# Strassen-like f16 matmul: the fault flag summed by a one-column TensorE product instead of a GpSimd all-reduce, with all instructions in a newly searched order

## The chip, the cores and the metric

One core of one Trainium2 chip. The metric is the device time of the whole program in microseconds (us). Engines are named PE (TensorE), DVE (VectorE), ACT (ScalarE), POOL (GpSimd) and SP (SyncE, which issues the DMAs). Before the change three runs gave a median of 1486.29 us (1484.29 to 1486.7).

## The reference

```
B, S, D = 8, 2048, 2048        # x: (8, 2048, 2048) f32, w: (2048, 2048) f32
cs = np.cumsum(x, axis=1)
diff = cs - concatenate([zeros, cs[:, :-1, :]], axis=1)
return np.matmul(diff, w)
```

The difference of a running sum is the input again, so what is computed is x·w: 16384 rows of 2048 by a 2048×2048 matrix, with f32 results.

## The kernel before

The kernel multiplies in f16 and adds in f32. The rows of x are cut into 128 tiles of 128 rows. The first 4 tiles are done as plain products while w is loaded and cast; the sums and differences of w's blocks that the rest needs are made after that. The other 124 tiles go in 31 **groups** of 4 (`group`, L554 to L648), and each group is a multiplication of 2×2 blocks with seven products instead of eight. Six of them, P1 to P5 and P7, are split once more in the same way (class `Seven`), into seven slots, P1.0 to P1.6 and so on. The sixth block product is done whole, in eight parts (P6g and P6h, L525 to L541). A **piece** is one slot or one such part: 4 matmuls of 128×128 by 128×512, in the source lines L435 to L448 (`quarter`) or L531. A group has 50 pieces.

Around the pieces of a group stand:

- on SP: loads of the next group's x (L134, into three stages of F), transposes of the cast tiles by DMA (`turn`, L162), and stores of finished results (`put`, L510, and in halves in the last group, L522);
- on ACT: casts of x to f16 (`narrow`), sums of absolute values for the range check (`weigh`, L152), and copies from PSUM (L118): in each of P1 to P5 and P7 `first` copies the bank of slot 0 to the bank in which slot 3 goes on, `out2` and `out4` copy partial results to SBUF, and `keep` copies a product into a result tile;
- on DVE (all in L115): the f16 sums of x blocks (S1g to S4h for the group, `s1` to `s4` in each product), the f16 sums of w blocks (`in1.Q1` and so on, 128×2048), and the f32 adds of PSUM banks onto results, such as C11h+P2.1 or C21h+P7.0;
- on POOL (also L115): f32 adds of SBUF tiles, 12 per group, such as P2.last, P7.last and C22g+C21.0. All 372 are of one form, 128×512.

In slot 1 a product needs `s1` and its `Q1`; in slot 2 it needs `s2`, and the copy `first` must have read the bank, because slot 2 adds to the bank that `first` copies from. P1.first overwrites a bank that C21h+P7.0 of the group before still reads. P5.first overwrites a bank that the C11 adds (C11g+P2, C11h+P2) still read.

The helpers don't issue at once. `record` (L97) notes each instruction with a label; `emit` (L103 to L111) sorts all of them by group number × 100000 + a place, and issues them in that order through `after` (L85), engine by engine. Each engine works its own queue in order. The places stand in the table `places` (L715 to L1155), one part for each of the first three and last three groups and one, with the key None, for groups 3 to 27. So that table is the schedule of all five engines.

After the last group, seven small DVE instructions (flag1 to flag7, L687 to L697) judge from the range sums whether f16 was enough. Flag8 (L702) makes the greatest value over all 128 partitions with GpSimd's `partition_all_reduce`; flag9 (L708, DVE) turns it into one number. L1159 loads that number into a register, and L1160 branches on it: when it is above 0 a general path with scaled inputs computes everything again. In these runs the general path is not taken.

Of the kernel before, what the change touches and what calls it, by code (L numbers as in the profile page):

```python
# [10 lines left out]
def kernel(  # L11
# [6 lines left out]
    nc = tc.nc  # L18
    P = 128
# [8 lines left out]
    f16 = mybir.dt.float16  # L28
# [30 lines left out]
    flags = tiny[:, 16:32]  # L59
    told = const.tile([P, 2, END - PLAIN], f16, name="told")  # L60
# [122 lines left out]
    record("zeros", "dve", lambda: nc.vector.memset(zeros, 0.0))  # L183
    record("ones", "dve", lambda: nc.vector.memset(number[0], 1.0))
# [495 lines left out]
    fault = tiny.bitcast(i32)[:, 40:41]  # L680

    def dve(label, ask):
        record(label, "dve", ask)

    def judge():
# [12 lines left out]
        dve("flag7", lambda: ins.tensor_scalar(flags[:, 3:4], seen_w, WLEAST, None, ALU.is_ge))  # L698
        record(
            "flag8",  # L700
            "pool",
            lambda: nc.gpsimd.partition_all_reduce(  # L702
                flags[:, 4:6], flags[:, 2:4], P, bass_isa.ReduceOp.max
# [4 lines left out]
            lambda: ins.tensor_scalar(  # L708
                fault, flags[:, 4:5], 1.0, flags[:, 5:6], ADD, ALU.is_gt
            ),  # L710
# [13 lines left out]
            'first x.0.0': -460890, 'ones': -457444, 'numbers': -438705,  # L724
            'numbers turned': -433943, 'first x.0.3': -422332, 'first x.1.0': -413922,
# [510 lines left out]
```

## Time and profile before

| | |
|---|---|
| median of three runs | 1486.29 us |
| profiled execution | 1483.12 us, of which the span is 1481.3 us |
| PE busy | 1430.6 us (97%), 6542 matmuls |
| DVE busy | 1328.8 us (90%) |
| ACT busy | 1043.6 us (70%) |
| POOL busy | 568.5 us (38%) |
| mean granted clock of PE | 0.991 |

The span runs from the first instruction to the last. The profile gives each engine's busy time, a picture of the span in 40 slices, the waits (who waited, for whom, total, times and longest), and rows in order of time: start in us, length in us, engine, line, operation, output, inputs, how many instructions the row joins, and in brackets the idle time before it with what ended it. A row "x4" of PE is one piece. Ends of matmuls are modelled and overlap the next start a little, so the pace of PE is read from the starts.

### The profile page before, as it was taken

The page shows a single profiled execution, that of the slowest core. Times are in us where ns is not written, and L with a number is a line of the kernel's source. Part 1 is how long each engine was busy: PE and PEld are TensorE (multiplying, and loading weights), DVE is VectorE, ACT ScalarE, POOL GpSimd, SP SyncE. Part 2 cuts the span into 40 slices and gives each one's busy share as a digit, 9 for nine tenths or more (in the row PEclk, how much of TensorE's full clock was granted, in tenths as well). Part 3 has the DMA queues.
Part 4 walks back from the last instruction along what each step waited for, and adds up shares of the span by engine and source line. Part 5 has one row for each costly group of instructions (what it writes and reads, how often), then busy time and mean ns, then how long its engine had stood idle before and what let it go on. Part 6 is the DMA issues. An engine that isn't in the chain of part 4 may idle for free. (4 is left out here: it accounts for less than half of the span.)

```text
span 1481.3 us, 20480 instructions
## 1 busy us (share of the span) xinstructions
PE 1430.6 (97%) x6542; PEld 630.3 (43%) x6542; DVE 1328.8 (90%) x2105; ACT 1043.6 (70%) x1716; POOL 568.5 (38%) x377
## 2 busy tenths in 40 slices
PE   8989999999999999999999999999999999999995
PEld 4434344444444444444444444444444444444442
DVE  2889889999999999999999999999999999998994
ACT  5976867767767777777777776777776776776761
POOL 0014432345443345443345443245443345443333
PEclk9999999999999999999999999999999999999997
DMA  9998788888888998878989988989888899878862
GB/s 359 355 220 246 211 221 236 245 245 230 236 227 244 242 256 232 238 229 231 248 248 244 224 232 233 230 254 245 227 231 236 245 249 240 226 223 231 242 190 93
DMA packets 343791, 351.63 MB, mean 237 GB/s; under 512 B 270976, under 2 KB 270976, under 8 KB 343680
## 3 DMA queue, kind: packets, MB, share of 16 engines
q1 hardware_dynamic: 343680, 350.29, 84.8%
q8 instruction: 52, 0.85, 0.2%
q14 instruction: 59, 0.48, 0.1%
HBM read 150.99 MB, written 134.22 MB: 193 GB/s over the span
## 5 line engine op out<-in xcount | busy, mean ns | idle before, releaser
L115 POOL TENSOR_TENSOR arena<-arena 128x512 f32<-128x512 f32 x372 | 567.9, 1542 | 901.3 <-DVE arena L115 427.0
L118 ACT COPY arena<-b 128x512 f32<-128x512 f32 x729 | 405.3, 589 | 247.0 <-PE b L438 179.4
L438 PE MATMUL b<-W,x 128*128 128x512 f16 x2108 | 517.3, 380 | 8.4 <-ACT arena L118 5.3
L438 PEld LDWEIGHTS <-x 128*128 128x128 f16 x3224 | 313.3, 98 | 412.1 <-issue 40.4
L115 DVE TENSOR_TENSOR arena<-W 128x2048 f16<-128x2048 f16 (+1 forms) x287 | 352.0, 1227 | 9.5 <-PE b L438 5.8
L438 PE MATMUL b<-W,arena 128*128 128x512 f16 x1364 | 338.4, 380 | 11.9 <-ACT b L118 9.5
L438 PEld LDWEIGHTS <-arena 128*128 128x128 f16 x1984 | 187.6, 98 | 271.5 <-DVE arena L115 36.9
L118 ACT CAST F<-F 128x1024 f16<-128x1024 f32 x248 | 257.1, 1047 | 57.6 <-DMA F<-in_x_dram 55.5
L438 PE MATMUL b<-arena,x 128*128 128x512 f16 x1116 | 282.4, 380 | 14.1 <-ACT arena L118 12.7
L115 DVE TENSOR_TENSOR arena<-arena,b 128x512 f32<-128x512 f32 x372 | 249.7, 680 | 30.0 <-PE b L438 11.9
L152 ACT ACTIVATE F<-F 128x1024 f16<-128x1024 f16 x248 | 264.4, 1067 | 1.0
L115 DVE TENSOR_TENSOR x<-x,x 128x1024 f16<-128x1024 f16 x372 | 227.9, 626 | 33.3 <-PE b L438 26.6
L531 PE MATMUL b<-W,x 128*128 128x512 f16 x992 | 240.3, 380 | 0.6 <-ACT F L152 0.4
L118 ACT COPY b<-b 128x512 f32<-128x512 f32 x186 | 106.5, 573 | 105.6 <-DVE arena L115 65.1
L438 PE MATMUL b<-arena 128*128 128x512 f16 x620 | 159.2, 379 | 3.0 <-DVE arena L115 2.4
L115 DVE TENSOR_TENSOR b<-b,arena 128x512 f32<-128x512 f32 x217 | 150.4, 693 | 4.6 <-PE b L438 1.2
L531 PEld LDWEIGHTS <-x 128*128 128x128 f16 x992 | 96.9, 98 | 118.2 <-DVE x L115 1.7
L115 DVE TENSOR_TENSOR arena<-b,arena 128x512 f32<-128x512 f32 x155 | 106.2, 686 | 27.9 <-PE b L438 17.7
L115 DVE TENSOR_TENSOR arena<-arena,x 128x512 f16<-128x512 f16 x124 | 80.5, 649 | 1.1
L115 DVE TENSOR_TENSOR x<-x 128x512 f16<-128x512 f16 x124 | 64.7, 522 | 2.4 <-PE b L438 1.2
L115 DVE TENSOR_TENSOR arena<-x,arena 128x512 f16<-128x512 f16 x124 | 64.1, 517 | 2.1 <-PE b L438 1.9
L115 DVE TENSOR_TENSOR arena<-x 128x512 f16<-128x512 f16 x124 | 58.4, 471 | 1.8
(40 smaller groups left out, 309.8 us busy)
## 6 DMA issues: line engine op xcount, KB each, us to landing
F<-in_x_dram SPq DMA_DIRECT2D x248, 512.0 KB, 5.1
out_dram<-arena SPq DMA_DIRECT2D x240, 512.0 KB, 5.2
W<-in_w_dram SPq DMA_DIRECT2D x32, 512.0 KB, 9.0
out_dram<-arena SPq DMA_DIRECT2D x32, 256.0 KB, 3.0
W<-in_x_dram SPq DMA_DIRECT2D x16, 256.0 KB, 7.7
x<-F SPq DMA_TRANSPOSE x248, 3.4
```

What stands on the lines that cost most here:

```text
L115: record(label, engine, lambda: on.tensor_tensor(dst, p, q, op))
L118: record(label, "act", lambda: nc.scalar.copy(to, p))
L152: return nc.scalar.activation(other, data, ABS, accum_out=m)
L438: said = nc.tensor.matmul(to, a[:, ds(k * P, P)], b[:, k, :], start=(start and k == 0), stop=(k == 3), skip_group_check=True,)
L531: said = nc.tensor.matmul(to[n], half(t, 0)[:, k, :], T2[k][:, n, :], start=False, stop=(k == KH - 1), skip_group_check=True,)
```

## The change

It has two parts. First, the flag: a vote of each partition is worked out on DVE from flags 2 and 3 (-256 for a partition that has seen a fault, +1 for one whose w was large enough). One PE matmul with a column of ones adds the 128 votes into one element of PSUM bank `xy[1][0]`. Flag9 compares this sum with 0.5. GpSimd takes no part in it, and `fault` is made on partition 0 only.

```
+    one = tiny.bitcast(f16)[:, 84:85]
...
+    record("one", "dve", lambda: nc.vector.memset(one, 1.0))
...
-    fault = tiny.bitcast(i32)[:, 40:41]
+    fault = tiny.bitcast(i32)[0:1, 40:41]
+    vote = tiny.bitcast(f16)[:, 86:87]
+    votes = xy[1][0]
...
+        dve(
+            "vote",
+            lambda: ins.tensor_scalar(
+                vote, flags[:, 2:3], -2.0 * P, flags[:, 3:4], MUL, ADD
+            ),
+        )
         record(
             "flag8",
-            "pool",
-            lambda: nc.gpsimd.partition_all_reduce(
-                flags[:, 4:6], flags[:, 2:4], P, bass_isa.ReduceOp.max
+            "pe",
+            lambda: nc.tensor.matmul(
+                votes[0:1, 0:1], one, vote, start=True, stop=True, skip_group_check=True
             ),
         )
         dve(
             "flag9",
-            lambda: ins.tensor_scalar(
-                fault, flags[:, 4:5], 1.0, flags[:, 5:6], ADD, ALU.is_gt
-            ),
+            lambda: ins.tensor_scalar(fault, votes[0:1, 0:1], 0.5, None, ALU.is_lt),
         )
```

Second, the whole table `places` is replaced. Before there were 6464 recorded instructions, now there are 6466: two more on DVE, one more on PE and one fewer on POOL. Two of the table's lines as they were:

```
-            'zeros': -4646627, 'warm.0': -4646625, 'warm.1': -4646623, 'warm.2': -4646621,
-            'warm.3': -4646618, 'warm.4': -4646616, 'warm.5': -4646614, 'warm.6': -4646612,
```

What this moves, at three places.

POOL's whole queue of the main path, before. L115 are its adds, L702 is flag8; "ISA" is an instruction that the compiler puts ahead of a change of kind, and x366 joins equal rows:

```order
L115 ISA
L115 TENSOR_TENSOR arena<-arena 128x512 x366
L702 ISA
L702 ISA tiny<-tiny 128x2
L115 ISA
L115 TENSOR_TENSOR arena<-arena 128x512 x6
L1159 TENSOR_LOAD tiny
L1160 COMPARE_AND_BRANCH
```

And now, with the two rows ahead of it (all lines of the helpers have moved down by one):

```order
L1236 MEMSET const-uint8-127 128x1
L1247 UNCONDITIONAL_BRANCH
L116 ISA
L116 TENSOR_TENSOR arena<-arena 128x512 x372
L1175 TENSOR_LOAD tiny
L1176 COMPARE_AND_BRANCH
```

The reduction stood between the adds of the last group, with six of them behind it. Now the 372 adds follow each other.

DVE at the hand-over from one middle group to the next, before. In order of the rows: P4.s4, the add P4.middle, C21g+P4.0, P1.s2 of the next group, C21h+P7.0, in1.Q1 (from W), C21g+P4.1, P1.s4, P1.middle:

```order
L115 TENSOR_TENSOR x_67<-x_67 128x512
L115 TENSOR_TENSOR b_81<-b_79,arena 128x512
L115 TENSOR_TENSOR arena<-arena,b_80 128x512
L115 TENSOR_TENSOR arena<-arena,x_62 128x512
L115 TENSOR_TENSOR arena<-arena,b_74 128x512
L115 TENSOR_TENSOR arena<-W 128x2048
L115 TENSOR_TENSOR arena<-arena,b_81 128x512
L115 TENSOR_TENSOR arena<-x_62,arena 128x512
L115 TENSOR_TENSOR b_75<-b_77,arena 128x512
```

Now, in order: P4.s4, C21g+P4.0, in1.Q1, C21h+P7.0, P1.s2, C21g+P4.1, P1.s3, C21h+P4.0, P1.middle, P1.s4:

```order
L116 TENSOR_TENSOR x_67<-x_67 128x512
L116 TENSOR_TENSOR arena<-arena,b_80 128x512
L116 TENSOR_TENSOR arena<-W 128x2048
L116 TENSOR_TENSOR arena<-arena,b_74 128x512
L116 TENSOR_TENSOR arena<-arena,x_62 128x512
L116 TENSOR_TENSOR arena<-arena,b_81 128x512
L116 TENSOR_TENSOR arena<-x_62,x_64 128x512
L116 TENSOR_TENSOR arena<-arena,b_78 128x512
L116 TENSOR_TENSOR b_75<-b_77,arena 128x512
L116 TENSOR_TENSOR arena<-x_62,arena 128x512
```

C21h+P7.0 (the row with b_74) and in1.Q1 stood behind P1.s2 and stand ahead of it now. On PE, P1.2 stood ahead of P1.1 (P2.0, P1.2, P1.1, P1.3) and stands behind it now (P2.0, P1.1, P1.2, P1.3).

DVE at the entry to P5 of a middle group, before. In order: C11h+P2.1, C11g+P2.1, C11h+P2.0, S1h, P5.s1, P5.s2, S2h, in5.Q1:

```order
L115 TENSOR_TENSOR arena<-arena,b_81 128x512
L115 TENSOR_TENSOR arena<-arena,b_79 128x512
L115 TENSOR_TENSOR arena<-arena,b_80 128x512
L115 TENSOR_TENSOR x_68<-x_68,x_69 128x1024
L115 TENSOR_TENSOR arena<-x_68 128x512
L115 TENSOR_TENSOR arena<-arena,x_66 128x512
L115 TENSOR_TENSOR x_64<-x_68,x_64 128x1024
L115 TENSOR_TENSOR arena<-W 128x2048
```

Now, in order: C11h+P2.1, S1h, S2h, P5.s1, C11g+P2.1, C11h+P2.0, P5.s2, in5.Q1:

```order
L116 TENSOR_TENSOR arena<-arena,b_81 128x512
L116 TENSOR_TENSOR x_68<-x_68,x_69 128x1024
L116 TENSOR_TENSOR x_64<-x_68,x_64 128x1024
L116 TENSOR_TENSOR arena<-x_68 128x512
L116 TENSOR_TENSOR arena<-arena,b_79 128x512
L116 TENSOR_TENSOR arena<-arena,b_80 128x512
L116 TENSOR_TENSOR arena<-arena,x_66 128x512
L116 TENSOR_TENSOR arena<-W 128x2048
```

S1h, S2h and P5.s1 have moved ahead of two of the adds that read the banks of P2. On PE, 18 pieces stand from P1.2 to the one ahead of P5.2, before and now.

On SP, turn7.0 (a transpose of this group's last tile) and the loads around it are moved by a place or two, and at the start the two loads w.0.1 and w.0.0 stand first, where x.0.1 stood first.

More of the change, by code (lines that the diff above doesn't have):

```diff
@@ L716 @@
         0: {
[7 rows of a table removed]
-            'first x.0.0': -460890, 'ones': -457444, 'numbers': -438705,
-            'numbers turned': -433943, 'first x.0.3': -422332, 'first x.1.0': -413922,
[153 rows of a table removed]
-        },
[47 rows of a table removed]
-        },
[45 rows of a table removed]
[7 rows of a table added]
+            'numbers': -648116, 'first x.1.0': -635524, 'first x.2.3': -593898,
+            'first x.0.1': -583215, 'first x.0.3': -573021, 'cast w.0.1': -565802,
+            'first x.0.2': -513040, 'first x.1.1': -509724, 'numbers turned': -509328,
[157 rows of a table added]
+        },
[47 rows of a table added]
+        },
[46 rows of a table added]
         },
         28: {
[44 rows of a table removed]
[44 rows of a table added]
         },
         29: {
[44 rows of a table removed]
[44 rows of a table added]
         },
         30: {
[41 rows of a table removed]
[42 rows of a table added]
         },
         None: {
[44 rows of a table removed]
[45 rows of a table added]
         },
```

851 rows, old and new, of the table places are left out of this document.

## The prediction

> **What bounds the kernel now.** I read the page first, from its top.
>
> ```profile
> span 1481.3 us, 20480 instructions
> PE 1430.6 (97%) x6542; PEld 630.3 (43%) x6542; DVE 1328.8 (90%) x2105; ACT 1043.6 (70%) x1716; POOL 568.5 (38%) x377
> PE   8989999999999999999999999999999999999995
> PEclk9999999999999999999999999999999999999997
> ```
>
> TensorE (PE) is busy 97% of the span at nearly full clock, with VectorE (DVE) at 90% behind it. So the kernel can only get shorter where PE stands idle, or where the end waits for somebody else; 1481.3 − 1430.6 = 50.7 us of idle PE is all there is. The last slice has a busy share of 5 and a clock of 7: the end is worse than the rest. Next the waits (engine and line, what it waited for, total, times, longest).
>
> ```profile
> PE b L438 <- ACT arena L118: 18.4, 10, 11.1
> DVE arena L115 <- POOL arena L115: 11.7, 1, 11.7
> PE b L438 <- ACT b L118: 10.5, 25, 0.9
> POOL arena L115 <- issue: 7.1, 1, 7.1
> POOL tiny L702 <- issue: 5.6, 1, 5.6
> ```
>
> Two things stand out. Single waits of 11 to 12 us on PE and DVE, beside the two long "issue" waits of GpSimd (POOL). And one wait that comes 25 times and costs 10.5 us: with 31 groups, that is one in nearly every group. The windows tell how the two are spread (start, length, busy time of PE and so on, clock, DMA share).
>
> ```profile
> 160.00:1300.00 1140.00, 1121.24 (x5119) 493.13 (x5118) 1059.28 (x1662) 821.12 (x1366) 476.35 (x310) 1.00 0.87 237
> 1460.00:1482.00 22.00, 3.71 (x9) 0.99 (x7) 5.50 (x9) 0.58 (x1) 7.96 (x7) 0.56 0.31 109
> ```
>
> In the long middle PE loses 1140 − 1121.24 = 18.8 us in 1140, which is 0.7 us per group of 44. In the last 22 us it works 3.7.
>
> **The end: the flag leaves GpSimd.** The rows of the last stretch, start and length first:
>
> ```profile
> 1450.95 3.95 POOL L115 TENSOR_TENSOR arena<-arena 128x512 f32<-128x512 f32 x3 [2.50 <-DVE arena L115]
> 1456.74 1.07 ACT L118 COPY arena<-b 128x512 f32<-128x512 f32 x2 [2.85 <-PE b L438]
> 1459.11 1.03 PE L438 MATMUL b<-W,arena 128*128 128x512 f16 x4
> 1460.52 0.37 POOL L702 PARTITION_ALL_REDUCE tiny<-tiny  x1 [5.61 <-issue]
> 1467.97 7.67 POOL L115 TENSOR_TENSOR arena<-arena 128x512 f32<-128x512 f32 x6 [7.08 <-issue]
> 1469.26 0.69 DVE L115 TENSOR_TENSOR arena<-arena,b 128x512 f32<-128x512 f32 x1 [11.68 <-POOL arena L115]
> 1471.28 1.87 PE L438 MATMUL b<-arena,x 128*128 128x512 f16 x4 [11.15 <-ACT arena L118]
> 1474.96 0.69 DVE L115 TENSOR_TENSOR arena<-arena,b 128x512 f32<-128x512 f32 x1 [1.02 <-PE b L438]
> 1475.57 0.21 DVE L708 TENSOR_SCALAR tiny<-tiny 128x1 int32<-128x1 f32 x1
> ```
>
> POOL finishes its adds at 1454.90, then stands 5.61 us before the reduction, works 0.37, and stands 7.08 us before its next adds. No data is named for either wait, and the matmuls that feed the next add were long done. So the switch to the reduction and back keeps POOL from adding for 1467.97 − 1454.90 = 13.07 us. DVE's C21g+P4.0 waits for POOL's first add there, because both touch the same tile; ScalarE (ACT) waits for DVE, and PE's last two pieces wait for ACT: 11.15 us.
>
> The Trainium skill, "GPSIMD Engine Reference", section 2.1 Instruction dispatch, says that the first call to a freshly loaded GpSimd kernel pays about 6 us with no instruction shown; the 5.61 and 7.08 here agree. Its section 4.1 Engine selection advises GpSimd for a reduction along partitions, which speaks against this change; the 13.07 us of the rows above outweigh it in this place, and by that advice the time would stay as it is.
>
> In the new order POOL has no instruction of another kind, so its six adds go on as their inputs come. The first needs C21g+P7.0, done by 1454.9. The second needs an ACT copy of P7, the first of the pair at 1456.74, done near 1457.3; the other four stand behind it. Five adds of 7.67 / 6 = 1.28 us from there end at 1463.7. PE's last two pieces follow 1460.13 directly, 0.86 each at full clock, and DVE's last add of 0.69 ends near 1462.6. So POOL's chain is what is late next, at 1463.7, where 1475.65 stood: **−11.9 us** (−11 if one add waits for an input, −13.07 if all inputs are early). What follows the last add until the end of the span, 1481.3 − 1475.65 = 5.65 us of stores and the branch, stays as long. What is added: two small DVE instructions, each at most the 0.21 us of the flag row above, and one matmul of one column, between 0 and the 0.43 us that one 512-column matmul takes at the slow clock of the end (1.87 is four of them). The flag's last step is put earlier, so its 0.21 goes from the end of DVE. I take all of this as 0; without cover it would be 0.8.
>
> **The group, first place: the wait at P1.2.** The rows at one hand-over between groups:
>
> ```profile
> 742.87 1.03 PE L438 MATMUL b<-W,x 128*128 128x512 f16 x4
> 747.82 2.68 POOL L115 TENSOR_TENSOR arena<-arena 128x512 f32<-128x512 f32 x2
> 749.26 1.52 DVE L115 TENSOR_TENSOR arena<-arena,x 128x512 f16<-128x512 f16 x1
> 750.64 1.03 PE L438 MATMUL b<-W,x 128*128 128x512 f16 x4
> 750.70 0.67 DVE L115 TENSOR_TENSOR arena<-arena,b 128x512 f32<-128x512 f32 x1
> 751.41 0.57 ACT L118 COPY b<-b 128x512 f32<-128x512 f32 x1 [0.66 <-DVE arena L115]
> 752.03 1.02 PE L438 MATMUL b<-W,arena 128*128 128x512 f16 x4 [0.36 <-ACT b L118]
> 752.89 1.03 PE L438 MATMUL b<-arena 128*128 128x512 f16 x4
> 757.03 0.42 DVE L115 TENSOR_TENSOR arena<-arena,x 128x512 f16<-128x512 f16 x1
> 786.91 1.03 PE L438 MATMUL b<-W,x 128*128 128x512 f16 x4
> ```
>
> The first and last rows are P1.0 of two groups: the period is 786.91 − 742.87 = 44.04 us. The nine pieces from 742.87 to 750.64 took 7.77 us, 0.863 each, so the 50 pieces of a group need 43.2, and 0.86 us per group is lost. More than half of it is here: P1.2 starts 752.03 − 750.64 = 1.39 after the piece before it, 0.52 too late. It waits for an ACT copy, that for DVE's C21h+P7.0 (750.70), and that stood behind P1.s2 (749.26), which took 1.52 us. The same form takes 0.42 at 757.03. The long one began while POOL was adding (747.82 to 750.50) and ended 0.28 after POOL: DVE was blocked 1.10 us.
>
> The Trainium skill, "SBUF — State Buffer", section Who interferes with whom, has the rule: a DVE instruction with both inputs in SBUF contends with a GpSimd one that reads SBUF, and "Issue order, not op shape, decides who blocks." The trace agrees, with 1.52 beside 0.42.
>
> The new order has C21h+P7.0 ahead of P1.s2, and puts P1.1 ahead of P1.2 on PE, so the copy is early by a piece and by the blocked add. What would be late next at this place is P1.1, which needs P1.s1 and in1.Q1, both now earlier on DVE. So this wait goes: 25 groups of its 25 waits by 0.52 = **−13 us**.
>
> **The group, second place: a wait at P5.2 that comes.** In the new order S1h, S2h and P5.s1 go ahead of the two adds C11g+P2.1 and C11h+P2.0 on DVE. The copy P5.first needs those adds, and P5.2 needs the copy. Rows of before around it:
>
> ```profile
> 754.02 0.70 DVE L115 TENSOR_TENSOR b<-b,arena 128x512 f32<-128x512 f32 x1
> 760.34 1.24 SPq L162 DMA_TRANSPOSE x<-F  x1
> 764.04 1.28 DVE L115 TENSOR_TENSOR arena<-arena,b 128x512 f32<-128x512 f32 x2
> 765.48 0.69 DVE L115 TENSOR_TENSOR arena<-arena,b 128x512 f32<-128x512 f32 x1 [0.16 <-PE b L438]
> 766.09 0.69 DVE L115 TENSOR_TENSOR x<-x,x 128x1024 f16<-128x1024 f16 x1
> 767.80 1.03 PE L438 MATMUL b<-W,arena 128*128 128x512 f16 x4
> 768.21 1.22 DVE L115 TENSOR_TENSOR arena<-W 128x2048 f16<-128x2048 f16 x1
> x<-F SPq DMA_TRANSPOSE x248, 3.4
> ```
>
> From P1.middle (754.02) to in5.Q1 (768.21) DVE takes 14.19 us for 23 instructions. Of these the new order has C21h+P4.0 (about 0.60 from start to start) and P1.s3 (0.33) ahead of that stretch and P5.s2 (0.33) behind it, and P1.s4 (0.33) in it: 14.19 − 0.93 = 13.26. P1.middle can start 1.73 after P1.2 does (1.02 for the piece, 0.58 for ACT's copy, and the hand-overs). With 0.57 for the copy P5.first and 0.05 each side, P5.2 can start 1.73 + 13.26 + 0.67 = 15.66 after P1.2. PE has 18 pieces in between, 18 × 0.863 = 15.54. That is a margin of −0.1 us: none. Whatever DVE loses in that stretch is now lost by PE. The likeliest loss is the one seen above: POOL's add P2.last comes just there, after C11h+P2.1, and P5.s1 and S1h have both inputs in SBUF; if POOL starts first, 1.10 us.
>
> A second chain arrives at the same place. S1h needs the transposed tile of turn7.0, issued at 760.34; at the median 3.4 us it landed at 763.7, 2.3 us ahead of S1h at 766.09. The two adds, the second of the pair at 764.04 and the one at 765.48, took 766.09 − 764.68 = 1.4 in front of S1h. Without them 0.9 is left, and more than half of that goes when the 0.52 at P1.2 goes. A late landing then delays S1h, P5.s1, the adds behind them, and PE.
>
> So the price of this place lies between 0 (DVE always first) and 0.1 + 1.10 = 1.2 us per group. I take about the middle, 0.5, by the nearest row (a block of 1.10 that falls in about half of the groups): 25 × 0.5 = **+13 us**. The two places cancel.
>
> **Start and transition.** The order of the first loads changes too: two loads of w come first, x.0.1 later.
>
> ```profile
> PE b L214 <- DVE W L205: 5.1, 1, 5.1
> 60.00:140.00 80.00, 74.19 (x339) 32.51 (x337) 74.23 (x113) 55.82 (x93) 19.20 (x13) 1.00 0.95 248
> ```
>
> PE's wait of 5.1 us is for the first cast tile; it moves by the landing of a load or two more or fewer ahead of that tile, by my estimate up to 2 us either way (a bit under half of the wait): the queue moves the same bytes. In the transition to the groups, PE idles 80 − 74.19 = 5.8 us; a new order there may win or lose most of it, ±4. I take 0 for both.
>
> **Sum.** The profiled execution took 1483.12 us, 1.8 more than its span. 1483.12 − 11.9 − 13 + 13 + 0 = 1471.2. The median of the three runs shown, 1486.29, lies 3.17 above that execution; the same sum from it is 1474.4. I forecast **1474.5 us**.
>
> **Rivals.**
> - *P5.2 never waits* (chance 0.22). DVE is first at P5.s1 in every group and turn7.0 is in time. Then the 13 us stay won: 1461.5. For it: DVE's own margin is only 0.1 short. Against it: the order repeats in every group, and so did the late copy at P1.2, 25 times. The rule quoted above from the Trainium skill, "SBUF — State Buffer", section Who interferes with whom, would give this result wherever P5.s1 issues before P2.last.
> - *P5.2 waits at the full price* (0.20), the slower side. If POOL is first each time and turn7.0 is late, each group gains 0.52 and loses 1.2: 25 × 0.68 = +17, less 11.9, gives 1491.5. It decides from a price of 0.52 + 11.9 / 25 = 1.0 us per group; by more than 0.2% from 1.12. For it: two chains end at that place with no margin. Against it: a PE that waits lets DVE and the loads catch up.
> - *The end isn't freed* (0.10). The change doesn't do what it says if POOL's stand of 13 us is a wait for something the views do not name, or if the new transition takes its gain: within 0.2%, 1486.
>
> **How the numbers follow.** The forecast, with P5.2 at about half price, has 0.48. A difference of 0.2%, about 3 us, is what a measurement of this kernel can tell from no change. Faster by more than that: 0.48 + 0.22 = 0.70; within it 0.10; slower 0.20. The range runs from the first rival less 2.5 us for the start, 1459, to the second, 1492; the tails beyond hold some 2 in 10. The forecast's own part, with the bounds of the end (−11 to −13), the start and the transition, is about 1468 to 1481.
>
> **What would show it.** No PARTITION_ALL_REDUCE, no "issue" wait of POOL over 1 us at the end, and the last PE piece within 2 us of the one before: the end is right; then 12 us less between POOL's last three adds and the end. The wait of PE for ACT b L118 falls from 25 times to a few: the first place is right. A wait of PE at P5.2, for ACT's copy, in about half the groups and a period near 44.0: the second is right; a period of 43.5 or less says the first rival, 44.7 or more the second. I am wrong altogether if the last PE piece still waits 11 us, or if the group's loss sits at a piece I have not named.

## The result, and the profile after

The changed kernel took 1467.42 us (median of four runs, 1465.45 to 1468.53), beside 1485.29 us for the kernel before in the same comparison: a ratio of 0.9878 with a 95% interval of 0.9861 to 0.9895, 17.9 us less. The forecast was 1474.5 in a range of 1459 to 1492; the direction and the range held, the gain was 6 us larger than forecast.

The top of the page of the changed kernel:

```profile
span 1463.4 us, 20495 instructions
PE 1426.9 (97%) x6543; PEld 631.4 (43%) x6543; DVE 1319.0 (90%) x2107; ACT 1050.7 (72%) x1716; POOL 531.5 (36%) x376
PE   8989999999999999999999999999999999999997
PEclk9999999999999999999999999999999999999999
```

The last slice has a busy share of 7 where it had 5, and its clock is full. Two of its waits over the whole span (total, times, longest):

```profile
PE b L440 <- ACT b L119: 7.3, 10, 1.2
PE b L440 <- ACT arena L119: 6.6, 5, 4.3
```

The wait for the ACT copies from bank to bank (ACT b) has fallen from 25 times to 10, and a single one is now up to 1.2 us. The longest wait of PE for ACT was 11.1 us; it is 4.3 now, and no longer at the end.

To see where the 17.9 us come from, the span is cut at a piece ahead of which both orders have done the same work: P2.0, behind which no piece of the group before is left. Its rows in groups 4 and 27, of before and of the changed kernel:

```profile
264.14 1.03 PE L438 MATMUL b<-W,x 128*128 128x512 f16 x4
...
1283.31 1.03 PE L438 MATMUL b<-W,x 128*128 128x512 f16 x4
```

```profile
265.76 1.03 PE L440 MATMUL b<-W,x 128*128 128x512 f16 x4
...
1277.45 1.03 PE L440 MATMUL b<-W,x 128*128 128x512 f16 x4
```

Up to group 4: 265.76 − 264.14 = +1.6 us. Groups 4 to 27: 1011.69 beside 1019.17, −7.5. From there to the end of the span: 185.95 beside 197.99, −12.0. Together −17.9, which is the difference of the spans, 1481.3 − 1463.4. (Both profiled executions lie about 2 us under the medians of their kernels.)

The end of the changed kernel:

```profile
1447.95 1.27 POOL L116 TENSOR_TENSOR arena<-arena 128x512 f32<-128x512 f32 x1 [0.16 <-DMA out_dram<-arena]
1450.55 7.90 POOL L116 TENSOR_TENSOR arena<-arena 128x512 f32<-128x512 f32 x6 [1.33 <-DVE arena L116]
1450.57 0.16 PE L712 MATMUL b<-tiny 128*1 128x1 f16 x1
1451.80 1.89 PE L440 MATMUL b<-arena,x 128*128 128x512 f16 x8 [1.07 <-ACT arena L119]
1455.25 1.03 PE L440 MATMUL b<-W,x 128*128 128x512 f16 x4
1458.48 0.69 DVE L116 TENSOR_TENSOR arena<-arena,b 128x512 f32<-128x512 f32 x1 [1.76 <-POOL arena L116]
```

The flag's matmul takes 0.16 us. POOL's six adds follow one another, and DVE's last add waits 1.76 us for POOL: POOL's chain is what is late next, as the prediction had it.

Counted from P2.0 of group 27, DVE's last add now ends at 1459.17 − 1277.45 = 181.72 us, and before at 1475.65 − 1283.31 = 192.34, which is 10.6 more. The other 1.4 of the 12.0 lie behind that add: 1463.4 − 1459.17 = 4.2 us, where it was 5.65.

### The profile page after: what moved, and what is told of

Same layout as the page of the kernel before. It is cut to its first block, busy times and chain, and to the rows that moved or that the text cites. A ratio compares the mean times of both kernels' runs of the same rounds, so it can differ in the third digit from the quotient of the medians.

```text
span 1463.4 us, 20495 instructions
## 1 busy us (share of the span) xinstructions
PE 1426.9 (97%) x6543; PEld 631.4 (43%) x6543; DVE 1319.0 (90%) x2107; ACT 1050.7 (72%) x1716; POOL 531.5 (36%) x376
## 5 line engine op out<-in xcount | busy, mean ns | idle before, releaser
L116 POOL TENSOR_TENSOR arena<-arena 128x512 f32<-128x512 f32 x372 | 531.3, 1445 | 926.7 <-DVE arena L116 728.2
L119 ACT COPY arena<-b 128x512 f32<-128x512 f32 x729 | 411.5, 590 | 267.9 <-PE b L440 197.0
L440 PE MATMUL b<-W,x 128*128 128x512 f16 x2108 | 526.6, 380 | 0.9 <-ACT b L119 0.4
L116 DVE TENSOR_TENSOR arena<-W 128x2048 f16<-128x2048 f16 (+1 forms) x287 | 359.9, 1255 | 45.0 <-PE b L440 44.6
L440 PE MATMUL b<-W,arena 128*128 128x512 f16 x1364 | 340.2, 379 | 9.4 <-ACT b L119 6.9
L440 PEld LDWEIGHTS <-arena 128*128 128x128 f16 x1984 | 192.5, 98 | 254.5 <-DVE arena L116 22.1
L440 PE MATMUL b<-arena,x 128*128 128x512 f16 x1116 | 286.0, 380 | 6.7 <-ACT arena L119 6.3
L533 PE MATMUL b<-W,x 128*128 128x512 f16 x992 | 240.5, 379 | 4.1 <-DVE x L116 2.9
L116 DVE TENSOR_TENSOR x<-x,x 128x1024 f16<-128x1024 f16 (+1 forms) x372 | 222.9, 607 | 12.2 <-PE b L440 3.3
L533 PEld LDWEIGHTS <-x 128*128 128x128 f16 x992 | 94.7, 98 | 128.3 <-DVE x L116 17.8
L116 DVE TENSOR_TENSOR arena<-x 128x512 f16<-128x512 f16 x124 | 73.3, 591 | 0.1
L116 DVE TENSOR_TENSOR arena<-x,x 128x512 f16<-128x512 f16 x124 | 62.4, 503 | 3.7 <-PE b L440 1.4
L254 PE MATMUL b<-W,arena 128*128 128x512 f16 x240 | 54.8, 379 | 2.6 <-ACT W L119 2.4
```

Source lines behind the costliest of these rows:

```text
L116: record(label, engine, lambda: on.tensor_tensor(dst, p, q, op))
L119: record(label, "act", lambda: nc.scalar.copy(to, p))
L254: said = nc.tensor.matmul(to[n], xP[:, r, ko, :], b[:, n, :], start=(ko == 0), stop=(ko == KO - 1))
L440: said = nc.tensor.matmul(to, a[:, ds(k * P, P)], b[:, k, :], start=(start and k == 0), stop=(k == 3), skip_group_check=True,)
L533: said = nc.tensor.matmul(to[n], half(t, 0)[:, k, :], T2[k][:, n, :], start=False, stop=(k == KH - 1), skip_group_check=True,)
```

## The experiments

Losses at a piece of PE are worked out here from the starts of all its pieces in a trace: a start later than 0.8635 us after the one before counts with what it is later by. "The groups" are 4 to 27, 24 in number; where a wait in single groups is told without rows, it comes from the same working.

**The two parts apart.** The flag alone: the first part of the change on the kernel before, with the old table and three places added:

```
+    places[0]["one"] = places[0]["zeros"] + 1
+    places[30]["vote"] = places[30]["flag6"] + 1
+    places[30]["flag8"] = places[30]["P4.3"] + 1
```

> The old order, with the flag summed by the TensorE product alone. If POOL's stand around the reduction held the end, the whole gain of the end is here: 11 to 12 us less than before, about 1474, with no wait of PE over 1 us at the end, and the wait of PE at P1.2 of 0.52 still in 25 groups. The rival, that the end was freed by the new order of the last group and not by the flag, expects less than 4 us.

It took 1471.69 us beside 1484.3, a ratio of 0.9918 (0.9901 to 0.9935): −12.6 us. Its POOL rows at the end:

```profile
1450.31 6.22 POOL L116 TENSOR_TENSOR arena<-arena 128x512 f32<-128x512 f32 x4 [2.50 <-DVE arena L116]
1456.77 6.52 POOL L116 TENSOR_TENSOR arena<-arena 128x512 f32<-128x512 f32 x5 [0.24 <-ACT arena L119]
1462.09 0.69 DVE L116 TENSOR_TENSOR arena<-arena,b 128x512 f32<-128x512 f32 x1 [0.53 <-POOL arena L116]
```

The "issue" waits of 5.61 and 7.08 us are gone, and PE's wait of 11.15 with them. From P2.0 of group 27 (1282.25) to the end of DVE's last add it takes 180.53 us, 11.8 less than before, and what follows stays as long (5.7 us). The wait at P1.2 stayed, with its 25 times:

```profile
PE b L440 <- ACT b L119: 10.0, 25, 0.7
```

The order alone: the changed kernel with the old flag8 and flag9 on GpSimd and DVE, at these places:

```
+    places[30]["flag8"] = places[30]["vote"]
+    places[30]["flag9"] = max(places[30].values()) + 1
```

> The new order, with the flag left to GpSimd between the same two adds as before, and its last step at the end of DVE. If the two parts add up, this keeps POOL's stand of 13 us and PE's long wait at the end, and gains only what the groups gain: 6 to 8 us less than before, about 1478. The rival, that the order hides the stand behind other work, expects 12 us or more less.

It took 1479.28 us, a ratio of 0.996 (0.9947 to 0.9973): −5.0 us, a little under the 6 to 8 expected. Its POOL rows show the stand again, unhidden:

```profile
1463.21 0.37 POOL L703 PARTITION_ALL_REDUCE tiny<-tiny  x1 [5.67 <-issue]
1470.65 7.68 POOL L116 TENSOR_TENSOR arena<-arena 128x512 f32<-128x512 f32 x6 [7.07 <-issue]
```

Each of the two stands begins, in the trace of the kernel before and in this one, with two instructions MODIFY_POOL_CONFIG (from 1454.87 and from 1460.85 before), ahead of the reduction and ahead of the adds behind it, where POOL's queue has its "ISA" rows. In the changed kernel there are none after the first microsecond.

12.6 and 5.0 make 17.6 of the 17.9: within the intervals the parts add up.

**The second place: why P5.2 waits.** Two groups of the changed kernel, one after the other, DVE, POOL and PE at the entry to P5. In the first, S1h waits for the transpose:

```profile
454.92 1.42 DVE L116 TENSOR_TENSOR x<-x,x 128x1024 f16<-128x1024 f16 x2 [0.40 <-DMA x<-F]
455.76 1.70 POOL L116 TENSOR_TENSOR arena<-arena 128x512 f32<-128x512 f32 x1 [4.31 <-ACT arena L119]
456.25 1.49 DVE L116 TENSOR_TENSOR arena<-x 128x512 f16<-128x512 f16 x1
459.59 1.02 PE L440 MATMUL b<-W,arena 128*128 128x512 f16 x4 [1.08 <-ACT b L119]
...
499.21 1.41 DVE L116 TENSOR_TENSOR x<-x,x 128x1024 f16<-128x1024 f16 x2
500.53 1.56 POOL L116 TENSOR_TENSOR arena<-arena 128x512 f32<-128x512 f32 x1 [4.30 <-ACT arena L119]
500.54 0.42 DVE L116 TENSOR_TENSOR arena<-x 128x512 f16<-128x512 f16 x1
```

In the second group P5.s1 and POOL's P2.last begin 0.01 us apart, P5.s1 takes 0.42, and POOL's add takes the longer time. In the first, the transpose turn7.0 landed late, S1h stood 0.40, P5.s1 came 0.49 behind POOL, and took 1.49. P5.2 lost 1.24 there. So the trace suggests a chain: late landing, then second place behind POOL, then 1.07 us on top. Six groups of 24 have a P5.s1 of 1.5 us, one more has a long S2h in its place. These seven are, in this trace, just the groups in which turn7.0 took 4.49 us or more from issue to landing; in the others it took 4.24 or less, and P5.2 lost nothing. Two experiments take the links apart.

The landing, by putting a store out of the transpose's way (in the changed order SP issues put2.0, put2.1, turn7.1 and turn7.0 one after the other):

```
+    places[None]["put2.0"] = places[None]["turn7.0"] + 1
```

> The changed kernel, with the store put2.0 issued behind the transpose turn7.0 and not ahead of it, in groups 3 to 27. If the waits at P5.2 come where turn7.0 lands late, there is less ahead of it in the queues, it lands up to 1 us earlier, and the 8 groups with a wait of about 1 us at P5.2 fall to 0 to 2: 5 to 8 us less than the changed kernel, about 1460. The rival, that POOL's start beside P5.s1 decides by itself, expects the same number of waits and 1467.

It took 1458.39 us, a ratio of 0.9825 (0.9807 to 0.9843) to the kernel before, 9 us less than the changed kernel, or 8 by the two ratios to the kernel before (0.9825 and 0.9878). The loss in the groups fell by 7.4 us, 6.9 of it from this place. Turn7.0 now needs 3.06 to 3.6 us from issue to landing in 23 of the 24 groups and 4.79 in one, where it needed 3.31 to 5.52. In 23 groups P5.2 doesn't wait. One wait is left:

```profile
PE b L440 <- ACT b L119: 1.0, 1, 1.0
```

It isn't in the group with the 4.79, whose transpose landed 13.44 us after P2.0, just in time. It is in group 5, where turn7.0 took 3.08 but was issued 10.77 us after P2.0 (8.65 to 9.65 in the other groups), and so landed at 13.85. What counts is when the tile lands, and not how long the transfer takes.

The block, by taking POOL's add away:

```
-        plus("P2.last", C11h[:, 1, :], lz, "pool")
+        if period[0] not in range(3, 28):
+            plus("P2.last", C11h[:, 1, :], lz, "pool")
```

> The changed kernel without POOL's add P2.last in groups 3 to 27 (that part of the result is left out). If a late turn7.0 alone made the wait, the waits at P5.2 stay at 0.9 to 1.3 us in about 8 groups. If the lateness is small and POOL's add, which then stands first, blocks P5.s1 and makes most of it, P5.s1 takes 0.42 in all groups, and what is left at P5.2 is under 0.3 us in most: 5 to 8 us less than the changed kernel.

It took 1453.82 us (one run). In seven groups S1h still waits for a late landing (4.65 to 4.86 us), but such a group looks so:

```profile
452.02 1.42 DVE L116 TENSOR_TENSOR x<-x,x 128x1024 f16<-128x1024 f16 x2 [0.43 <-DMA x<-F]
453.36 0.42 DVE L116 TENSOR_TENSOR arena<-x 128x512 f16<-128x512 f16 x1
...
455.62 1.02 PE L440 MATMUL b<-W,arena 128*128 128x512 f16 x4
```

P5.s1 takes 0.42 in every group, and the loss at P5.2 falls to 0.21 in two of them. So lateness alone costs almost nothing, and with the tile in time the block didn't occur in the groups: it takes both. (The 13.6 us gained are more than this place: in the groups 10.8 went, 7.6 of them here and 1.7 at P4.1.)

**The first place: why P1.2 waited.** The old order with one pair exchanged on DVE:

```
+    places[None]["P1.s2"] = places[None]["P1.first"] - 1
```

> The kernel before, with one pair exchanged on DVE in groups 3 to 27: C21h+P7.0 ahead of P1.s2. If P1.s2, blocked by POOL's add, holds the copy P1.first and so P1.2, this alone takes the 0.52 at P1.2 out of the groups: 11 to 13 us less than before, about 1472. The rival, that P1.2 would wait for P1.s2 itself or that the loss only moves to another piece, expects less than 4 us.

It took 1490.1 us, a ratio of 1.0047 (1.0031 to 1.0063): 7 us slower, where 11 to 13 less were expected. The wait at P1.2 is gone in all groups, and P1.1, the next piece, is late by 0.7 to 0.8:

```profile
751.82 6.30 POOL L115 TENSOR_TENSOR arena<-arena 128x512 f32<-128x512 f32 x4
753.85 0.92 DVE L115 TENSOR_TENSOR arena<-arena,x 128x512 f16<-128x512 f16 x1
754.59 1.03 PE L438 MATMUL b<-W,x 128*128 128x512 f16 x4
754.79 2.19 DVE L115 TENSOR_TENSOR arena<-W 128x2048 f16<-128x2048 f16 x1
755.45 1.03 PE L438 MATMUL b<-W,arena 128*128 128x512 f16 x4
756.91 0.67 DVE L115 TENSOR_TENSOR arena<-arena,b 128x512 f32<-128x512 f32 x1
757.04 1.02 PE L438 MATMUL b<-arena 128*128 128x512 f16 x4 [0.56 <-DVE arena L115]
```

In1.Q1 (754.79) takes 2.19 us where its form takes 1.22. P1.s2 (753.85) is still held up by the add that it met before, though for less (0.92 us and not 1.52). New is the add behind that one, C22h+C21.0. It needs C21h+P7.0. In the kernel before it waited for it ("0.96 <-DVE" at 751.45) and began 0.15 us behind in1.Q1 (751.30); now that C21h+P7.0 is done earlier, POOL runs on and begins this add 0.26 to 0.39 us ahead of in1.Q1. So the exchange put in1.Q1 behind POOL. To show that it is this and not the buffer that in1.Q1 waits for (it comes free after P4.6), one of POOL's next adds was left out, and then both:

```
-                plus(f"C22{s}+C21.{i}", v[:, i, :], c[:, i, :], "pool")
+                if s == "g" or i == 1 or period[0] not in range(2, 28):
+                    plus(f"C22{s}+C21.{i}", v[:, i, :], c[:, i, :], "pool")
```

> The old order with C21h+P7.0 ahead of P1.s2 in groups 3 to 27, and without POOL's add C22h+C21.0 in groups 2 to 27 (that part of the result is left out). If the wait that came at P1.1 is in1.Q1 blocked behind that add, in1.Q1 takes 1.2 us and not 2.2, the wait of 0.71 at P1.1 falls under 0.1, and the time goes below the kernel before by 8 us or more. If in1.Q1 is late because its buffer comes free only after P4.6, the wait at P1.1 stays above 0.3.

1487.99 us (one run), and no answer: the second add moved up into the place of the first, began 0.38 us ahead of in1.Q1, and in1.Q1 took 2.14. The next run drops `or i == 1` as well:

> As the run before it, but without both of POOL's adds C22h+C21.0 and C22h+C21.1 in groups 2 to 27 (left out of the result), because the second had stepped into the place of the first, 0.38 us ahead of in1.Q1. If the block by POOL's add makes the wait at P1.1, in1.Q1 now takes 1.2 us, P1.1 waits under 0.1, and the time falls by 15 us or more against the run before it. If in1.Q1 is late for its buffer, the wait of 0.7 stays above 0.3.

1476.9 us (one run). In1.Q1 takes 1.23 and P1.1 follows without a wait:

```profile
746.94 1.28 POOL L115 TENSOR_TENSOR arena<-arena 128x512 f32<-128x512 f32 x1
747.57 0.93 DVE L115 TENSOR_TENSOR arena<-arena,x 128x512 f16<-128x512 f16 x1
748.56 1.23 DVE L115 TENSOR_TENSOR arena<-W 128x2048 f16<-128x2048 f16 x1
...
750.09 1.03 PE L438 MATMUL b<-arena 128*128 128x512 f16 x4
```

The loss at P1.1 went from 16.8 us over the groups to none: the block made it, not the buffer. The time fell by 11.1 and not by 15 (one run each); 5.2 us came back at P1.5, P3.0 and P6g.1.0.

**The start.** PE's longest wait of the changed kernel, 4.3 us, is at P1.6 of group 0: on ACT the cast narrow3.1 waits for its load, ahead of the copy P1.out4 that P1.6 needs.

```profile
81.95 1.04 ACT L119 CAST F<-F 128x1024 f16<-128x1024 f32 x1 [1.98 <-DMA F<-in_x_dram]
83.53 1.87 PE L440 MATMUL b<-arena,x 128*128 128x512 f16 x4 [4.31 <-ACT arena L119]
85.20 3.62 PE L440 MATMUL b<-W,x 128*128 128x512 f16 x8
88.61 1.28 PE L440 MATMUL b<-W,arena 128*128 128x512 f16 x4
60.00:140.00 80.00, 73.88 (x324) 31.82 (x323) 71.42 (x110) 56.17 (x94) 18.42 (x12) 0.96 0.89 236
```

Behind this wait PE is slow as well. The three pieces from 83.53 to 88.61 take 1.7 us each and not 0.86, which is 2.5 us more; the granted clock of the window is 0.96 (1.00 in the same window before).

```
+    places[0]["narrow3.1"] = places[0]["out.1.2.0"] + 1
```

> The changed kernel, with the cast narrow3.1 of group 0 moved behind four copies on ACT. If PE's 4.3 us at P1.6 of group 0 come from that cast, which waits for its load ahead of P1.out4, the wait falls under 1 us. The stores that the copies wait for land near 83 us, so 1 to 3.5 us less than the changed kernel are expected: 1464 to 1466. The rival, that the landing of the stores sets the pace there whatever stands ahead, expects the same time, with the wait at P2.0.

It took 1465.03 us. That is 2.4 less than the changed kernel, but in this comparison the kernel before was 2.4 faster too (1482.89 beside 1485.29): the ratio is 0.988 (0.9859 to 0.9901) beside 0.9878. So no gain shows, and the rival was right in the time; the wait at P1.6 did fall under 1 us:

```profile
79.79 1.02 PE L440 MATMUL b<-arena,x 128*128 128x512 f16 x4 [0.43 <-ACT arena L119]
82.41 0.59 ACT L119 COPY arena<-b 128x512 f32<-128x512 f32 x1 [2.67 <-DMA out_dram<-arena]
83.05 1.44 PE L440 MATMUL b<-W,x 128*128 128x512 f16 x3 [2.23 <-ACT arena L119]
```

P1.6 waits 0.43, and then P2.0 waits 2.23 for a copy that waits for a store to land.

**Put together.** Three edits at once:

```
+    places[None]["put2.0"] = places[None]["turn7.0"] + 1
+    places[None]["P4.1"] = places[None]["P3.4"] + 1
+    places[0]["narrow3.1"] = places[0]["out.1.2.0"] + 1
```

> The changed kernel with put2.0 behind turn7.0, narrow3.1 of group 0 behind the four copies, and P4.1 behind P3.4 on PE in groups 3 to 27 (P4.1 waits 0.15 in each of them). If the three add up: 8 to 9 us for the first, 1 to 3 for the second, 25 times 0.15 = 3.7 for the third: 1452 to 1456. If the third only moves its wait to another piece: 1455 to 1459.

1468.39 us (0.9904, 0.9881 to 0.9927), which is 10 worse than the first edit alone, and 12 by the ratios. The wait of 0.15 at P4.1 became a loss of 0.62 at P7.1 in each of the groups, in the waits as

```profile
PE b L440 <- DVE arena L116: 11.0, 24, 0.5
```

In7.Q1 is written into the buffer that P4.1 reads, so P4.1 a piece later makes in7.Q1 later, and P7.1 with it. Without that edit:

> The changed kernel with two edits: put2.0 behind turn7.0 in groups 3 to 27, narrow3.1 of group 0 behind the four copies. The first alone took 9 us off the changed kernel, the second 2; if they add up, 1455 to 1458. If the group 0 edit only moves a wait, 1458 to 1460.

1458.98 us (0.9833, 0.9816 to 0.9849), the same as the store's edit alone with 1458.39. So the group 0 edit is worth nothing that shows, alone or beside the other, and the best version of the study is the changed kernel with put2.0 behind turn7.0, 26 us under the kernel before.

## Why the prediction was right in its range, and 6 us short

- **The end, forecast −11.9.** The flag alone measured −12.6, the trace −12.0 from P2.0 of group 27 on, of which 0.9 is that group's. The mechanism was right, with POOL's adds late next. With the flag alone the size was right too: the last add ends 11.8 earlier, and nothing changes behind it. In the changed kernel the last add gained only 10.6, and another 1.4 came from the stretch behind it, which the prediction held at 5.65; why it became shorter wasn't tried. So that the end of the changed kernel comes out at the forecast is in part luck. The rival that the end isn't freed fell with the flag alone, and the order doesn't hide the stand (second run).
- **The first place, forecast −13.** The loss at P1.2 fell from 13.4 us over the groups to 0.3: the size was right. The reason was too short. The prediction gave the exchange of C21h+P7.0 and P1.s2, and P1.1 ahead of P1.2; the exchange alone makes the kernel 7 us slower, because the block goes to in1.Q1. In the new order in1.Q1 stands ahead of both, begins 0.14 to 0.25 us ahead of POOL's add C22g+C21.1 in every group, and it is that add which takes 2.25 us and not 1.27; P1.1 isn't held. That this place of in1.Q1 is what frees P1.1 was not tried by itself.
- **The second place, forecast +13.** This is the term of the sum that was mis-sized. The place was right, and so was the price of one wait: 0.9 to 1.3 us in six groups and 1.5 in a seventh, where P6h.0.0 shares it. It came in 7 groups of 24 and not in half of them, 8.0 us in all. That half had been assumed from no row, and the count differs between executions: with the same order in the groups it was 7 in the trace of the start's edit, and 9 (12.3 us) in that of the order alone, its slowest run. Nor was DVE's margin −0.1 us: without POOL's add an S1h that began 0.51 late cost 0.21, and one 0.25 late nothing, so that some 0.3 are to spare. The prediction listed POOL's block and the late transpose as two causes that end at the same place. The runs showed that they are one: the transpose decides in which groups the block falls, and the block makes it dear. Without lateness P5.s1 and P2.last meet within 0.01 us in most groups, and DVE isn't blocked.
- **Small waits, not in the sum.** The rest of the loss in the groups fell from 14.4 us to 11.3: waits at P1.5, P4.5, P3.0 and P5.4 went, and 0.15 each at P6g.0.0 and P4.1 came. The prediction took the group's loss from one hand-over, 0.86 us with a period of 44.04; on average the period was 1019.17 / 23 = 44.31. It is 1011.69 / 23 = 43.99 now. By the prediction's sign, a period near 44.0, the half price would have been confirmed; with the true period before, the sign doesn't decide.
- **Start and transition, forecast 0 ± 4.** +1.6. The first plain product starts at 12.23 us and not at 15.79. The 4.3 us at P1.6 of group 0 and the 2.5 us of slow pieces behind it more than take that back; what else is in the +1.6 wasn't worked out.

Worked out again with what was measured: −11.1 for the end without group 27, in the 24 groups 13.2 gained, 8.0 paid and 3.1 gained, and 1.6 lost at the start: −17.8, beside the −17.9 measured. So the 6 us that the forecast was short are the second place (5.0) and the small waits (3.1), less 1.6 at the start and 0.8 at the end. The range, 33 us wide, also held the first rival, so that the time alone decides little between them. The rival in which P5.2 never waits, 1461.5, is what the store's edit then reached, at 1458.4.

## What to carry to other kernels

Here GpSimd stood 13 us for one instruction of another kind that took 0.37: look at the idle time on both sides of a lone instruction before its own length. Where two engines block each other, taking one victim out of the way gives the block to the next instruction in line, so judge an exchange by the whole stretch and not by the pair. And a wait that comes in some groups and not in others has a cause that varies: here a transfer's landing, which a store moved behind it in the queue made regular in nearly every group.

## What the runs showed of the hardware

- Who is first in a near tie: with POOL's add 0.01 us ahead, DVE went through in 0.42 and POOL's add took 1.56. In the kernel before, POOL's add was about 0.03 ahead (749.23, from 750.50 less one add of 1.27), and DVE took 1.52. Over the groups, DVE went through with POOL up to 0.015 us ahead, and was blocked from 0.023 on; the two places differ in more than this, so that a single point between is not shown.
- A blocked DVE instruction that takes 0.42 us when free ends 0.28 us after POOL's add, in both kernels: 457.74 after 457.46 (456.25 + 1.49, 455.76 + 1.70), and 750.78 after 750.50. The Trainium skill, "SBUF — State Buffer", section Who interferes with whom, has the one that issues first block the other; the rows agree, apart from the near tie above.
- POOL paid for the change of kind both ways, 5.61 us on the way to the reduction and 7.08 on the way back to the add that it had done 366 times. The Trainium skill, "GPSIMD Engine Reference", section 2.1 Instruction dispatch, speaks of the first call to a freshly loaded kernel; the 7.07 and 7.08 us here were paid on a return.
- A DMA transpose of the same size (turn7.0) took 3.31 to 5.52 us from issue to landing with the store put2.0 ahead of it, and 3.06 to 3.6 with the store behind it in 23 groups of 24, 4.79 in the other.
- With a column of ones as weights, one PE matmul of one column summed 128 partitions in 0.16 us.
